# The first x on two hardware queues: a batched matmul on one core

## The chip, the core and the metric

The kernel runs on one core of a Trainium2 chip. The metric is the device time of one execution in microseconds. "Before" is 514.33 us (median of 3 runs, 514.29 to 514.34). A ratio below is the mean time of one kernel's fast runs over the mean of the other's fast runs of the same rounds, so it is not quite the ratio of the medians that stand beside it.

## The reference

```python
batch, m, k, n = 32, 512, 1024, 768
x      = randn(batch, m, k)   # float32
weight = randn(batch, k, n)   # float32
return np.matmul(x, weight).astype(np.float32)
```

There are 32 independent products. x and the weights are 167.8 MB, the output is 50.3 MB.

## The kernel before

Row p of SBUF holds rows 4p to 4p+3 of a batch of x, so a "row tile" is one of four groups of 128 rows. x has to be transposed on PE before it can be multiplied. A transfer "lands" with the last increment of its semaphore, and a "ring" is one queue as a DMA engine sees it. Batch 0 is loaded in float32 from SyncE's hardware queue. All other x and all weights come from GpSimd's software queue, which casts them to bf16 on the way.

```python
x_pool = ctx.enter_context(tc.tile_pool(name="x", bufs=3))
w_pool = ctx.enter_context(tc.tile_pool(name="w", bufs=4))
# ... cut: other pools, views, load_pair, load_w (all on nc.gpsimd) ...

x_first = x_pool.tile([P, MT - 1, K], F32, name="x_sb")     # row tiles 0 to 2
x_fourth = one_pool.tile([P, 1, K], F32, name="one_sb")     # row tile 3
nc.sync.dma_start(x_first, x_view[0, :, :MT - 1])
few = [slice(at, first + 20, 4) for first in (0, 20, 40) for at in range(first, first + 4)]
for rows in (slice(64, 96), slice(96, 112), slice(112, P), slice(60, 62), slice(62, 64), *few):
    nc.sync.dma_start(x_fourth[rows, 0], x_view[0, rows, MT - 1])
load_w(0)
# ... cut: identity matrix ...
load_pair(1); load_w(1); load_w(2); load_pair(3)

for b in range(B):
    # ... cut: loads of x and stores of finished pairs, all on nc.gpsimd ...
    if b + AHEAD < B:                      # AHEAD = 3: waits until weight b-1 is used up
        load_w(b + AHEAD)
    if b == 0:
        xT = {mt: transpose_first(mt) for mt in range(MT - 1)}
    # ... cut: transposes of later batches ...
    for pair in range(2):
        pm = banks()
        for half in range(2):
            mt = 2 * pair + half
            if mt not in xT:               # the fourth tile of batch 0
                xT[mt] = transpose_first(mt)
            matmuls(pm, half, xT[mt], b, range(KT), False)
        evacuate(b, pair, pm)
```

The fourth tile is cut into 17 pieces. Its pieces of 5 rows (12 of them) and of 2 rows go to few DMA engines, which will matter below.

## Time and profile before

| what | before |
|---|---|
| median | 514.33 us |
| span in the profile | 512.6 us |
| PE busy | 84% of the span |
| DMA engines' packets, both queues | 100.6% of 16 engines' span |
| PE starts on x / first product / fourth tile | 10.22 / 15.87 / 42.90 us |
| weight 0 lands | 15.83 us |
| PE's waits for weights after 150 us | 28.7 us in 9 waits |
| last store: issued / last semaphore increment | 503.43 / 511.64 us |

The lines themselves are in the prediction.

### The profile page before, as it was taken

The numbers are of one execution on the slowest core, as the hardware profiler recorded it, in microseconds if no ns is written. First come the engines' busy times: TensorE is split into PE (matmuls) and PEld (weight loads), VectorE is DVE, ScalarE is ACT, GpSimd is POOL, SyncE is SP. The second block draws the span as 40 slices with busy tenths as digits, with TensorE's granted clock in tenths as the row PEclk, the third lists the DMA queues.
The fourth block names the chain that finished last, engine by engine and source line by source line (L and its number), as shares of the span: only waits on it lengthen the run. The fifth ranks groups of instructions, "written<-read, shape, count | busy, mean of one in ns | idle before, by whom it ended". The sixth has DMA issues, their size and how long they took to land.

```text
span 512.6 us, 5733 instructions
## 1 busy us (share of the span) xinstructions
PE 431.9 (84%) x2528; PEld 278.5 (54%) x2576; DVE 130.0 (25%) x196; ACT 76.2 (15%) x129; POOL 37.0 (7%) x69
## 2 busy tenths in 40 slices
PE   2806999999999996997979989897897979999992
PEld 1504666666666563664636546464464645666561
DVE  1203223241415140231413204151050410514130
ACT  1100121212121201111111101111111111111210
POOL 3000010101010101001010000101001000010000
PEclk9956999999999998998989979999798997999998
DMA  8999999999999999999999999999999999999998
GB/s 241 223 221 213 218 218 218 333 220 308 245 219 333 217 323 234 226 326 221 328 225 234 318 224 332 217 246 307 221 333 216 258 295 219 331 219 216 322 427 339
DMA packets 12136, 135.63 MB, mean 265 GB/s; under 512 B 1232, under 2 KB 1232, under 8 KB 2128
## 3 DMA queue, kind: packets, MB, share of 16 engines
q0 software_dynamic: 10864, 126.88, 96.5%
q1 hardware_dynamic: 1248, 8.39, 4.1%
q8 instruction: 20, 0.33, 0.2%
q14 instruction: 4, 0.03, 0.0%
HBM read 167.77 MB, written 50.33 MB: 426 GB/s over the span
## 4 chain that ended last, share of the span: by engine, by line
PE 46%; DMA 37%; issue 8%; DVE 5%; another core or an unknown queue 2%; POOL 1%; ACT 0%; SPq 0%; POOLq 0%
PE pm L123 40%; DMA w_sb<-in_weight_dram 29%; DMA one_sb<-in_x_dram 8%; PE pt L78 5%; DVE xT L85 4%; DVE out_sb L144 1%; PE pt L105 0%; POOL out_dram L164 0%; POOL x_sb L60 0%; POOL w_sb L70 0%; DVE one_sb L144 0%; DVE xT L93 0%; ACT out_sb L145 0%; SPq L151 0%
## 5 line engine op out<-in xcount | busy, mean ns | idle before, releaser
L123 PE MATMUL pm<-w_sb,xT 128*128 128x256 bf16 (+1 forms) x2000 | 349.7, 334 | 31.2 <-DMA w_sb<-in_weight_dram 28.7
L123 PEld LDWEIGHTS <-xT 128*128 128x128 bf16 x2048 | 204.6, 100 | 171.8 <-DMA w_sb<-in_weight_dram 32.2
L144 DVE COPY out_sb<-pm 128x512 f32<-128x512 f32 x62 | 42.9, 692 | 318.3 <-PE pm L123 318.3
L78 PE MATMUL pt<-ident,x_sb 128*128 128x128 f32 x496 | 79.8, 303 | 10.4 <-DVE xT L85 10.1
L78 PEld LDWEIGHTS pt<-ident,x_sb 128*128 128x128 f32 x496 | 69.3, 209 | 21.5 <-DVE xT L85 18.7
L85 DVE COPY xT<-pt 128x1024 bf16<-128x1024 bf16 x120 | 77.4, 687 | 11.0 <-PE pt L78 11.0
L143 ACT COPY out_sb<-pm 128x512 f32<-128x512 f32 x62 | 36.3, 585 | 267.4 <-PE pm L123 267.4
L145 ACT COPY out_sb<-pm 128x512 f32<-128x512 f32 x62 | 36.3, 585 | 151.1 <-PE pm L123 151.1
L70 POOL DMA_DIRECT2D w_sb<-in_weight_dram x33 | 18.0, 546 | 406.4 <-PE pm L123 405.6
L105 PE MATMUL pt<-ident,one_sb 128*128 128x128 f32 x8 | 1.9, 422 | 19.0 <-DMA one_sb<-in_x_dram 19.0
L106 DVE CAST xT<-pt 128x512 bf16<-128x512 f32 x8 | 5.9, 732 | 34.8 <-PE pt L105 34.3
L105 PE MATMUL pt<-ident,x_sb 128*128 128x128 f32 x24 | 5.8, 426 | 10.2 <-DMA x_sb<-in_x_dram 10.2
L105 PEld LDWEIGHTS pt<-ident,one_sb 128*128 128x128 f32 x8 | 1.6, 219 | 19.4 <-issue 19.4
L105 PEld LDWEIGHTS pt<-ident,x_sb 128*128 128x128 f32 x24 | 4.4, 214 | 11.2 <-issue 10.2
L164 POOL DMA_DIRECT2D out_dram<-out_sb x14 | 10.1, 719 | 0.4 <-issue 0.3
L60 POOL DMA_DIRECT2D x_sb<-in_x_dram x15 | 8.1, 539 | 11.2 <-PE pt L105 11.2
L144 DVE COPY one_sb<-pm 128x512 f32<-128x512 f32 x2 | 1.4, 692 | 9.0 <-PE pm L123 9.0
L93 DVE COPY xT<-pt 128x1024 bf16<-128x1024 bf16 x4 | 2.6, 686 | 0.2 <-PE pt L78 0.2
L145 ACT COPY one_sb<-pm 128x512 f32<-128x512 f32 x2 | 1.2, 586 | 4.2 <-PE pm L123 4.2
L143 ACT COPY one_sb<-pm 128x512 f32<-128x512 f32 x2 | 1.2, 585 | 3.8 <-PE pm L123 3.8
L143 ACT ACT_TABLE_LOAD x1 | 1.3, 1283 | 0.7 <-PEq L230 0.7
L64 POOL DMA_DIRECT2D x_sb<-in_x_dram x1 | 0.5, 536 | 0.0
(6 smaller groups left out, 0.9 us busy)
## 6 DMA issues: line engine op xcount, KB each, us to landing
w_sb<-in_weight_dram POOLq DMA_DIRECT2D x31, 1536.0 KB, 41.7
out_dram<-out_sb POOLq DMA_DIRECT2D x14, 3072.0 KB, 55.8
x_sb<-in_x_dram POOLq DMA_DIRECT2D x15, 2048.0 KB, 50.2
out_dram<-out_sb SPq DMA_DIRECT2D x2, 1536.0 KB
x_sb<-in_x_dram SPq DMA_DIRECT2D x1, 1536.0 KB
w_sb<-in_weight_dram POOLq DMA_DIRECT2D x2, 768.0 KB, 48.8
out_dram<-one_sb SPq DMA_DIRECT2D x2, 768.0 KB
out_dram<-out_sb SPq DMA_DIRECT2D x2, 768.0 KB
```

What stands on the lines that cost most here:

```text
L60: nc.gpsimd.dma_start(out=xs[b], in_=pair_view[b // 2])
L70: nc.gpsimd.dma_start(out=ws[b][:, at:at + n, :], in_=w_view[b, :, at:at + n, :])
L78: nc.tensor.transpose(pt[:, j, :], pairs[:, mo, j::JT], ident)
L85: nc.vector.tensor_copy(both[:, :, :, :, half, :].rearrange("p b j i r -> p j b i r"), words(b, mt + MT * half).rearrange("p j (b i r) -> ...
L93: nc.vector.tensor_copy(xT.rearrange("p j m r -> p (j m r)"), words(B - 1, mt).rearrange("p j m -> p (j m)"))
L105: nc.tensor.transpose(pt[:, i, :], rows[:, JT * h + i::KT], ident)
L106: nc.vector.tensor_copy(xT[:, 2 * h:2 * h + 2].rearrange("p j m r -> p j r m"), pt.rearrange("p (j r) m -> p j r m", r=2),)
L123: nc.tensor.matmul(pm[bank][:, at:at + size], xT[:, ko // 2, :, ko % 2], ws[b][:, ko, off:off + size], start=(ko == 0 and not (together an ...
L143: nc.scalar.copy(o[:, 0:512], pm[0])
L144: nc.vector.tensor_copy(o[:, 512:1024], pm[1])
L145: nc.scalar.copy(o[:, 1024:N2], pm[2])
L164: nc.gpsimd.dma_start(out=two_view[at], in_=twos[at])
```

## The change

The intent is to begin the first x on two hardware queues at once, so that PE can start on tile 0 sooner. Two pieces of the fourth tile are also merged.

```diff
-        nc.sync.dma_start(x_first, x_view[0, :, :MT - 1])
+        nc.scalar.dma_start(x_first[:, 1:], x_view[0, :, 1:MT - 1])
+        nc.sync.dma_start(x_first[:, 0], x_view[0, :, 0])
         few = [...]
-        for rows in (slice(64, 96), slice(96, 112), slice(112, P), slice(60, 62), slice(62, 64), *few):
+        for rows in (slice(64, 96), slice(96, P), slice(60, 62), slice(62, 64), *few):
             nc.sync.dma_start(x_fourth[rows, 0], x_view[0, rows, MT - 1])
```

## The prediction

> **What bounds the kernel now.** I read the page's summary first, then the busy time by stretches, then PE's waits after 150 us, then the opening of the timeline. The summary names the bound:
>
> ```profile
> PE 431.9 (84%) x2528; PEld 278.5 (54%) x2576; DVE 130.0 (25%) x196; ACT 76.2 (15%) x129; POOL 37.0 (7%) x69
> DMA  8999999999999999999999999999999999999998
> q0 software_dynamic: 10864, 126.88, 96.5%
> q1 hardware_dynamic: 1248, 8.39, 4.1%
> HBM read 167.77 MB, written 50.33 MB: 426 GB/s over the span
> ```
>
> PE is busy for 84%, but the 16 DMA engines are at 90% or more in every slice except the first and the last, and the two queues together took 96.5 + 4.1 = 100.6% of the engines' span (packets overlap slightly). The software queue is issued by GpSimd: all weights and all x from batch 1 on, with a cast to bf16 on the way. The hardware queue is SyncE's: batch 0's x and the last stores.
>
> Next the stretches (columns: stretch, length, busy us of each engine, granted clock, DMA share, GB/s on the SBUF side, where a cast counts as half of what HBM gave):
>
> ```profile
> 2.00:6.00 4.00, 0.00 (x0) 0.00 (x0) 0.00 (x0) 0.02 (x1) 3.09 (x7) 1.00 0.87 307
> 6.00:16.00 10.00, 5.78 (x25) 4.70 (x26) 3.67 (x5) 0.00 (x0) 0.00 (x0) 1.00 1.05 245
> 16.00:43.00 27.00, 7.91 (x49) 4.63 (x49) 1.43 (x2) 1.75 (x3) 0.53 (x1) 0.69 1.03 221
> 100.00:485.00 385.00, 345.53 (x2023) 221.68 (x2060) 102.87 (x156) 60.07 (x103) 27.79 (x48) 0.95 1.02 263
> 485.00:503.00 18.00, 17.33 (x107) 11.12 (x108) 4.45 (x8) 3.31 (x7) 0.00 (x0) 1.00 1.01 427
> ```
>
> From 2 us to 503 us DMA has no hole. In 16 to 43 us PE works 7.91 of 27 us and DMA still runs at 1.03: PE may stand still there without DMA running out of work. Each transfer lies in a long backlog:
>
> ```profile
> w_sb<-in_weight_dram POOLq DMA_DIRECT2D x31, 1536.0 KB, 41.7
> x_sb<-in_x_dram POOLq DMA_DIRECT2D x15, 2048.0 KB, 50.2
> ```
>
> A weight lands 41.7 us after its issue (the least of all is 14.6 us, for the first), although consecutive landings in the trace are only 7.3 us apart (3.15 MB of HBM reads, 431 GB/s). And the waits of PE from 150 us on:
>
> ```profile
> PE pm L123 <- DMA w_sb<-in_weight_dram: 28.7, 9, 5.5
> ```
>
> Nine waits, 28.7 us, the last until 423.7 us, when weight 26 lands. So PE follows DMA until 423.7 us, and after that DMA is still full: the last store is issued at 503.43 us and its last semaphore increment comes at 511.64 us, 8.2 us later, while 768 KB alone take 1.84 us at the pace of the landings there (507.94, 509.80, 511.64). Both ends of the tail hang on the DMA stream. The time is: start of the stream, plus its work, plus little.
>
> The opening, where the change is:
>
> ```profile
> 0.74 0.38 SPq L151 DMA_DIRECT2D x_sb<-in_x_dram  x1
> 1.27 0.68 POOL L70 DMA_DIRECT2D w_sb<-in_weight_dram  x1 [0.82 <-POOLq L230]
> 10.22 5.84 PE L105 MATMUL pt<-ident,x_sb 128*128 128x128 f32 x24 [10.22 <-DMA x_sb<-in_x_dram]
> 15.87 8.00 PE L123 MATMUL pm<-w_sb,xT 128*128 128x512 bf16 x47
> 42.90 1.94 PE L105 MATMUL pt<-ident,one_sb 128*128 128x128 f32 x8 [19.03 <-DMA one_sb<-in_x_dram]
> ```
>
> The transposes wait for all three row tiles until 10.22 us, because they come as one transfer with one semaphore. The first product, at 15.87 us, starts right after weight 0 lands (15.83 us). The fourth tile comes in 17 pieces and holds PE until 42.90 us.
>
> **What the Trainium skill says.** "DMA: Bandwidth & Descriptors", section "Issuing engines are not separate DMA queues": transfers from any issuer run on the same 16 engines and interleave; a second issuer saves only issue time. The trace agrees as far as it can: one full set of engines, and an issue of 0.38 us before 6 us of moving. The same page, "Queues, rings and completion order": each DMA engine takes turns between the queues at packet granularity. The trace agrees: from 8 to 16 us, while a weight packet takes 925 ns, each engine completes about one small hardware packet per weight packet. Same page, "Rules for kernel authors": "Doesn't help" stands against spreading DMAs over issuers for bandwidth. No run yet shows it here. "Perfetto Trace Analysis", section "DMA Optimizations", says that splitting transfers may finish a task sooner if the DMA engines are generally idle. In this trace they are not, so what it promises can hold only in the first 6 us. On the cost of small packets I go by the trace: 460 ns for 12,288 B and 159 to 172 ns for 4,096 B.
>
> **The change part by part.** Bytes do not change: 167.77 MB read, 50.33 MB written. The instruction order differs only in one issue more on ScalarE, before its table load, and one less on SyncE.
>
> *Issue.* SyncE's first issue took 0.38 us and ScalarE is free at the same 0.7 us. The first packet starts at 1.77 us now; one semaphore step of the start gates both engines, so it stays about there. Gain 0.0. The table load moves by some 0.4 us; ScalarE's first copy is at 18.60 us, so that is hidden.
>
> *More, smaller packets.* Batch 0's first three tiles were 128 packets of 12,288 B, 8 per DMA engine. They become 8 of 8,192 B and 8 of 4,096 B. From 234 ns for 6,144 B and 460 for 12,288 B, a packet costs about 8 ns plus 36.8 ns per KB; a packet after a change of queue seems to cost 13 ns more (172 against 159). That is 8 x (8 + 13), about 0.17 us per DMA engine, at most.
>
> *Ramp.* These 128 packets took 577 ns on average, against 460 at best, because until 5.84 us only this one queue runs (weight 0's first packet) and the rate there was 356 GB/s. The excess is 117 ns x 8 = 0.94 us per engine. If a second ring keeps more requests in flight, part of this can be won; all of it is the ceiling. If the excess is congestion of 16 engines starting at once, nothing is won. I take a third: 0.3 us.
>
> *The merged piece* (rows 96 to 128 in one instead of two transfers of 16 rows): one 22 ns semaphore packet less per engine. Nothing.
>
> *Order in the opening.* The two rings take turns, so tile 0 does not come three times sooner: 8 packets of each ring are done together, at about 6 to 7 us instead of 8.8, and with the 1.2 us to the semaphore PE begins at about 8 us, not 10.2. Weight 0 still lands at about 16, so the first product stays at about 15.9. The fourth tile's large pieces stand behind 0.5 MB instead of 1.5 MB, and part goes out before 5.84 us: about three turns of 1 us fewer, so PE resumes at about 40 us instead of 42.9. Both are PE time, in a stretch where PE is not the bound: weight 4 is issued at 48.78 us now behind a backlog that lasts until 68.10 us, so 3 us earlier moves no byte. PE waits that much longer at its DMA waits after 150 us.
>
> Sum: -0.3 (ramp) + 0.1 (packets) = -0.2 us. 514.33 - 0.2 = 514.1 us.
>
> **The rivals.** First, the early start of PE carries through: 2.9 us, or 0.6%, to 511.4 us. For it speaks only the chain of waits, which runs through the fourth tile at the start; against it the full DMA in 16 to 43 us and the nine later waits, which absorb any lead. Second, the second ring lifts the first 4 us to the steady rate: -0.9 us, 513.4. The 427 GB/s of the last stores, on one hardware ring, speak against one ring being the limit, but those write to HBM. Third, the rings hamper each other or delay weight 0: three queues in turn give it a third of the turns for a while. Weight 0 may be 1 us late, but then something else is 1 us early; the stream is as long. With the packet cost and a worse ramp I come to +0.5 us, 514.8.
>
> **Range and chances.** The ceiling of the gain and the worst of the packet cost give 513.4 to 514.8; 0.1 to 0.2 us more on each side for another chip or run: 513.3 to 515.0. Two per cent are 10.3 us, ten times all that the first x can cost; so within 2% is 0.98, and 0.01 for each side.
>
> **What would show it right or wrong.** Right: transposes from about 8 us, first product still near 16, the fourth tile's transposes near 40, DMA share 1.0 from 2 to 503 us, PE's waits for weights after 150 us grown by about the lead (28.7 to some 31), the last wait still ending at 423 to 424 us. Wrong on the ramp: the DMA share and GB/s in 2 to 6 us rise or fall clearly and every later landing shifts by the same. Wrong on the bound: PE's waits do not grow and the end moves by microseconds.

## The result, and the profile after

The changed kernel takes 514.38 us (median of 4 runs, 514.35 to 514.65), against 514.34 us of the kernel before in the same rounds. The ratio is 1.0002, with a 95% interval of 0.9984 to 1.0019: the same.

The summary of the changed kernel (busy us, DMA by slices, queues) has a third queue, q10, which is ScalarE's:

```profile
PE 435.2 (85%) x2576; PEld 278.3 (54%) x2576; DVE 129.8 (25%) x196; ACT 76.2 (15%) x129; POOL 37.0 (7%) x69
DMA  8999999999999999999999999999999999999998
q0 software_dynamic: 10864, 126.88, 96.5%
q1 hardware_dynamic: 1232, 7.34, 3.6%
q10 hardware_dynamic: 144, 1.05, 0.5%
```

The three queues sum to 100.6% again. The 3 us more of PE are not more work: 48 matmul records are missing in the trace of before (2528 against 2576).

The same stretches as in the prediction (100 to 485 us, again at a DMA share of 1.02 and 263 GB/s, is left out):

```profile
2.00:6.00 4.00, 0.00 (x0) 0.00 (x0) 0.00 (x0) 0.45 (x1) 3.10 (x7) 1.00 0.98 333
6.00:16.00 10.00, 5.42 (x26) 4.23 (x27) 4.16 (x6) 0.00 (x0) 0.53 (x1) 0.98 1.02 240
16.00:43.00 27.00, 10.35 (x54) 6.09 (x53) 0.71 (x2) 1.75 (x3) 0.00 (x0) 0.69 1.04 224
485.00:503.00 18.00, 16.43 (x104) 10.47 (x101) 4.65 (x7) 3.51 (x6) 0.00 (x0) 1.00 1.02 431
```

In the first stretch the rate seems to be up, from 307 to 333 GB/s. It is not: the view counts each DMA record in the stretch in which it starts, and ahead of 2.00 us the kernel before had started 12 records of 12,288 B, the changed one 8 of 4,096 B. Counted from 0 us, before and then after, the rates are alike:

```profile
0.00:6.00 6.00, 0.00 (x0) 0.00 (x0) 0.00 (x0) 1.28 (x1) 4.03 (x12) 1.00 0.71 229
0.00:6.00 6.00, 0.00 (x0) 0.00 (x0) 0.00 (x0) 1.28 (x1) 4.03 (x12) 1.00 0.70 227
```

From 6 to 16 us the rate is down from 245 to 240. From there on nothing differs that could move the end.

The opening of the changed kernel in order of time, and PE's waits after 150 us:

```profile
0.74 0.40 ACTq L151 DMA_DIRECT2D x_sb<-in_x_dram  x1
0.74 0.38 SPq L152 DMA_DIRECT2D x_sb<-in_x_dram  x1
8.97 3.65 PE L105 MATMUL pt<-ident,x_sb 128*128 128x128 f32 x16 [8.97 <-DMA x_sb<-in_x_dram]
15.56 9.64 PE L123 MATMUL pm<-w_sb,xT 128*128 128x512 bf16 x48 [1.40 <-DMA w_sb<-in_weight_dram]
41.85 1.94 PE L105 MATMUL pt<-ident,one_sb 128*128 128x128 f32 x8 [16.65 <-DMA one_sb<-in_x_dram]
```

```profile
PE pm L123 <- DMA w_sb<-in_weight_dram: 28.8, 10, 4.9
```

Both issues start at 0.74 us, as the change wants. PE starts on x 1.25 us sooner (8.97 against 10.22), then has a new wait of 1.40 us for weight 0, and the first product comes 0.31 us sooner. The fourth tile comes 1.05 us sooner. Of that, 0.7 us is left when weight 4 is issued (48.10 against 48.78 us), and none of it reaches a landing. The trace has the landing of every load and store of the software queue, and set side by side they show what became of it: weight 0 lands 0.31 us sooner than before, the next x 0.31 us later, from there to 115 us every transfer 0.2 to 0.3 us later, and those from 124 us up to 467 us between 0.04 us sooner and 0.2 us later. (The experiment with PE held back by 5 us, further down, has the opening of the kernel before, and from 124 us on its landings lie 0.4 us before to 0.6 us after those, so that differences of this size say nothing there.) At the last DMA wait of PE that both kernels share, the landing is at 423.70 us (before: 423.65).

The tail shows it once more. PE happened to finish 1.06 us sooner in this profile, so the last store was issued at 502.37 us instead of 503.43. Its last increment still came at 511.92 us, against 511.64.

### The profile page after: what moved, and what is told of

It reads as the page before. It is cut to its first block, busy times and chain, and to the rows that moved or that the text cites. A ratio compares the mean times of both kernels' runs of the same rounds, so it can differ in the third digit from the quotient of the medians.

```text
span 512.8 us, 5782 instructions
## 1 busy us (share of the span) xinstructions
PE 435.2 (85%) x2576; PEld 278.3 (54%) x2576; DVE 129.8 (25%) x196; ACT 76.2 (15%) x129; POOL 37.0 (7%) x69
## 3 DMA queue, kind: packets, MB, share of 16 engines
q10 hardware_dynamic: 144, 1.05, 0.5%
## 4 chain that ended last, share of the span: by engine, by line
PE 49%; DMA 36%; DVE 5%; issue 5%; another core or an unknown queue 2%; POOL 1%; SPq 0%; ACT 0%; POOLq 0%
PE pm L123 43%; DMA w_sb<-in_weight_dram 28%; DMA one_sb<-in_x_dram 6%; PE pt L78 5%; DVE xT L85 4%; DMA x_sb<-in_x_dram 2%; DVE out_sb L144 1%; PE pt L105 0%; POOL out_dram L165 0%; POOL x_sb L60 0%; POOL w_sb L70 0%; DVE one_sb L144 0%; DVE xT L93 0%; SPq L155 0%
## 5 line engine op out<-in xcount | busy, mean ns | idle before, releaser
L123 PE MATMUL pm<-w_sb,xT 128*128 128x256 bf16 (+1 forms) x2048 | 353.7, 336 | 30.2 <-DMA w_sb<-in_weight_dram 30.2
L78 PE MATMUL pt<-ident,x_sb 128*128 128x128 f32 x496 | 79.8, 302 | 10.5 <-DVE xT L85 10.2
```

Of the source, the lines that this page charges most:

```text
L78: nc.tensor.transpose(pt[:, j, :], pairs[:, mo, j::JT], ident)
L123: nc.tensor.matmul(pm[bank][:, at:at + size], xT[:, ko // 2, :, ko % 2], ws[b][:, ko, off:off + size], start=(ko == 0 and not (together an ...
```

## The experiments

There are two theories to tell apart. The first is the prediction's: the DMA stream sets the end, so PE's opening has slack, and who issues the first x does not matter. The rival is that PE's opening is on the path, as the chain of waits suggests, so that a better arrangement of the first x would pay.

### One queue instead of two (e1_one_queue)

```diff
 # against the changed kernel
-        nc.scalar.dma_start(x_first[:, 1:], x_view[0, :, 1:MT - 1])
         nc.sync.dma_start(x_first[:, 0], x_view[0, :, 0])
+        nc.sync.dma_start(x_first[:, 1:], x_view[0, :, 1:MT - 1])
```

> Tile 0 and then tiles 1 and 2 as two transfers, both from SyncE; the rest as in the changed kernel. Theory (the DMA stream sets the end, whoever issues): 514.3 to 514.5 us, as both kernels. On one ring the transfers go in order, so tile 0 lands well before 8.97 us, by an estimate from 0.5 MB at about 330 GB/s behind 1.77 us plus 1.2 us to the semaphore at about 4.6 us; PE starts there and the end does not move. If the second ring lifted the rate in 2 to 6 us (307 before, 333 after), it falls back to about 307 here; if the smaller packets did it, it stays at about 333. Rival (an earlier start of PE carries to the end): about 4 us faster than the changed kernel, near 510.

Measured: 514.53 us (514.41 to 514.70, 5 runs), before in the same rounds 514.52; ratio 1.0002 (0.9988 to 1.0016). The stretch from 0 to 6 us, and PE's opening:

```profile
0.00:6.00 6.00, 0.58 (x3) 0.61 (x4) 0.00 (x0) 1.28 (x1) 4.02 (x12) 1.00 0.71 224
5.42 1.94 PE L105 MATMUL pt<-ident,x_sb 128*128 128x128 f32 x8 [5.42 <-DMA x_sb<-in_x_dram]
11.23 3.90 PE L105 MATMUL pt<-ident,x_sb 128*128 128x128 f32 x16 [3.88 <-DMA x_sb<-in_x_dram]
15.75 9.86 PE L123 MATMUL pm<-w_sb,xT 128*128 128x512 bf16 x47 [0.62 <-DMA w_sb<-in_weight_dram]
```

Two things follow. For its own aim, the second queue is the worse choice: one queue serves its transfers in order, so PE has tile 0 at 5.42 us instead of 8.97; the two rings take turns, and there tile 0 lands (8.83 us) only 1.55 us before the two other tiles (10.38 us). And the test of the rate, 307 or 333 GB/s from 2 to 6 us, was none: this kernel has 328, but it too had started only 8 records of 4,096 B before 2 us, and from 0 to 6 us it moves 224 GB/s, no more than the 229 of the kernel before. PE's start 4.8 us before that of the kernel before moves nothing, because the first product waits for weight 0 (15.75 us).

### The merged piece alone (e3_merge_only)

```diff
-(slice(64, 96), slice(96, 112), slice(112, P), ...)
+(slice(64, 96), slice(96, P), ...)
```

> The kernel before with only the merged piece of the change: rows 96 to 128 in one transfer instead of two of 16. Theory: one semaphore packet of 22 ns less per DMA engine and one place fewer in the order of SyncE's issues: 514.3 to 514.5 us, fourth tile within 1.5 us of 42.9. No rival gives it more than 0.1 us.

Measured: 514.52 us (514.24 to 516.80, 6 runs) against 514.45 us; ratio 1.0007 (0.9993 to 1.0021). The merge is worth nothing that can be measured. The profile fell on an execution of 515.0 us span with a lower granted clock, and is of use for another reason:

```profile
core 0: 515.0 us, clock 0.842
PE 468.8 (91%) x2528; PEld 290.1 (56%) x2576; DVE 130.3 (25%) x196; ACT 76.2 (15%) x129; POOL 36.9 (7%) x69
PE pm L123 <- DMA w_sb<-in_weight_dram: 0.4, 1, 0.4
```

The last line is PE's waits from 100 us on. At a clock of 0.842 instead of 0.938 PE has next to no waits left and the kernel becomes PE-bound, yet it is only 2.4 us longer. PE is thus a close second bound. The same trace shows which of the two sets the end at the usual clock. PE's slower pace puts the issues of weights up to 17.3 us later than before, and up to 467 us no landing moves by more than 0.6 us. At the end the last store but one lands at 509.71 us (before: 509.79), DMA then stands still until the last store is issued at 510.81 us, and that one lands 3.25 us later, at 514.06. In the kernel before it lands 8.2 us after its issue, so PE could have been some 5 us later there (an estimate from these two figures). What the change did is read from the runs at the usual clock.

### PE held back by 5 and by 16 us (e4_pe_late_6us, e5_pe_late_24us)

These two touch no DMA. Idle transposes, whose result nobody reads, are put on PE after those of the fourth tile: 36 in the first kernel, 144 in the second.

```diff
                     if mt not in xT:
                         xT[mt] = transpose_first(mt)
+                        for _ in range(9):        # 36 in the second kernel
+                            idle = tpsum.tile([P, JT, P], F32, name="pt")
+                            for i in range(JT):
+                                nc.tensor.transpose(idle[:, i, :], x_fourth[:, 0, i::KT], ident)
```

> The kernel before with 36 idle transposes on PE after the fourth tile's, about 6.1 us at 0.17 us each (8 took 1.35 us in the trace), no DMA changed. Theory: the smallest slack of PE against the DMA backlog in this stretch is weight 5, issued at 64.86 us behind a landing at 75.39 us, so 10.5 us; 6 us less of it moves no byte: 514.3 to 514.5 us. Rival (PE's time at the start is on the path): 520.4.

> The same with 144 idle transposes, about 24.5 us. Theory: this exceeds the slack of 10.5 us by 14 us, DMA then runs dry, and the time grows by those 14 us plus some 1 to 4 us until the stream is full again: 528 to 533 us, and DMA share falls visibly between 60 and 100 us. Rival one (PE's start on the path from the first us): 538.8. Rival two (PE is never on the path): 514.4.

Measured: 514.49 us (514.37 to 514.78, 5 runs) for the small delay, ratio 1.0001 (0.9988 to 1.0013); 526.97 us (526.58 to 527.57, 4 runs) for the large one, ratio 1.0244 (1.0230 to 1.0258); before 514.52 us. The idle transposes, the issue of weight 5, and the stretch from 43 to 100 us, first of the small and then of the large delay:

```profile
44.87 5.97 PE L215 MATMUL pt<-ident,one_sb 128*128 128x128 f32 x36
69.80 0.53 POOL L70 DMA_DIRECT2D w_sb<-in_weight_dram  x1 [15.53 <-PE pm L123]
43.00:100.00 57.00, 55.35 (x336) 38.82 (x343) 16.62 (x25) 8.19 (x14) 4.61 (x8) 0.95 1.01 242
```

```profile
44.85 16.93 PE L215 MATMUL pt<-ident,one_sb 128*128 128x128 f32 x144
80.74 0.53 POOL L70 DMA_DIRECT2D w_sb<-in_weight_dram  x1 [15.54 <-PE pm L123]
43.00:100.00 57.00, 55.39 (x378) 43.19 (x384) 15.25 (x23) 5.85 (x10) 2.85 (x5) 0.97 0.88 178
```

The small delay moves the issue of weight 5 from 64.86 to 69.80 us and its landing by 0.06 us. The large one was less than planned (144 transposes took 16.9 us, 0.12 each, not 0.17), and still DMA ran dry: its share falls from 1.01 to 0.88, and weight 5 lands 8.63 us later. The time of 526.97 us is below the 528 to 533 I expected, for a delay that was a third smaller than planned.

This gives an estimate of the slack. Issued at 80.74 us into an empty queue, weight 5 landed at 91.28, so 10.54 us after its issue. In the kernel before it lands at 82.65 us, so by the same 10.54 us it could be issued as late as 72.1 us without loss: 7.3 us later than it is. No run has a delay between 5.2 and 13.4 us that would test it closer. I had reckoned 10.5 us, leaving out the time to fill an empty queue. The growth of 12.4 us is made of 8.6 us at weight 5, another 1.8 us at the x behind it, and some 2 us that come in later along the stream; the last part I cannot assign.

So both simple rivals fall. PE's opening is not on the path within a slack of about 7.3 us, and it is beyond.

### The stream started late (e7_stream_late)

```diff
+        nc.vector.memset(x_first, 0.0)
         nc.sync.dma_start(x_first, x_view[0, :, :MT - 1])
```

> The kernel before; VectorE first fills the tile of batch 0's first three row tiles with zeros, so that SyncE's first transfer has to wait for it. Nothing else moves. Theory: the stream's start counts one to one. With a fill of 2 to 4.4 us (estimate: 3072 columns at the pace of the 512-column casts, 0.73 us each, is 4.4 us at most) the first packet comes that much later than 1.77 us, but weight 0 still begins near 5.8 us; the stream loses the bytes of the hole, about 307 of 430 GB/s by time: +1.5 to +3.5 us, 515.8 to 517.9. Rival (the start is hidden by later waits): 514.4.

Measured: 523.71 us (522.33 to 523.77, 4 runs) against 514.45; ratio 1.0172 (1.0159 to 1.0186). My expectation, 515.8 to 517.9, was wrong. The fill, the issue, the first transposes, the first product, the fourth tile, and the stretch from 43 to 100 us:

```profile
1.45 2.62 DVE L151 MEMSET x_sb<- 128x3072 f32 x1 [1.45 <-PEq L231]
4.10 0.38 SPq L152 DMA_DIRECT2D x_sb<-in_x_dram  x1
21.53 5.43 PE L105 MATMUL pt<-ident,x_sb 128*128 128x128 f32 x24 [21.53 <-DMA x_sb<-in_x_dram]
26.80 7.96 PE L123 MATMUL pm<-w_sb,xT 128*128 128x512 bf16 x47
55.92 1.94 PE L105 MATMUL pt<-ident,one_sb 128*128 128x128 f32 x8 [21.16 <-DMA one_sb<-in_x_dram]
43.00:100.00 57.00, 42.52 (x250) 28.57 (x255) 15.92 (x24) 6.45 (x11) 2.86 (x5) 0.85 0.92 197
```

The x was issued only 3.4 us later, but PE started 11.3 us later. The trace says why: with no x in its way, weight 0's first packet starts at 2.65 us instead of 5.84, and lands 1.65 us sooner; the x, now second, starts at 7.74 us and shares the engines packet by packet with weight and x of the software queue until 19.9 us. The stream itself began only 0.88 us later (2.65 against 1.77). But PE's delay was 13.4 us at weight 5, more than the slack of 7.3 us: by the number of the previous experiment it should land 13.4 - 7.3 = 6.1 us later, and it landed 6.10 us later (again it was issued into an empty queue, and landed 10.47 us after its issue). The rest of the 9.3 us comes in as in the experiment before: 1.3 us at the next x and some 2 us along the stream. Holding x back thus cost little by the stream and much by PE. It also corrects one reading of mine: weight 0 is late in the opening because x is before it, not because its own start takes that long.

### The fourth tile in one transfer (e6_fourth_whole)

```diff
-        for rows in (slice(64, 96), slice(96, 112), slice(112, P), slice(60, 62), slice(62, 64), *few):
+        for rows in (slice(0, P),):
```

> The kernel before with the fourth row tile in one transfer of 128 rows instead of 17 pieces. PE then starts on it soon after 16 us instead of 42.9: a lead of some 25 us. Theory (DMA bound): the lead is lost in the later waits for weights, which grow from 28.7 us to about 54. The 60 rows that went to few DMA engines are spread over all 16, so the others carry 4 packets of 172 ns more: +0.7 us, 515.0. Rival (PE's start on the path): 489.

Measured: 515.97 us (515.77 to 516.52, 5 runs) against 514.45; ratio 1.0029 (1.0016 to 1.0042). The fourth tile, the first wait of PE for a weight, and all such waits from 28 us on:

```profile
23.57 1.04 PE L105 MATMUL pt<-ident,one_sb 128*128 128x128 f32 x8
33.65 16.64 PE L123 MATMUL pm<-w_sb,xT 128*128 128x512 bf16 x99 [0.21 <-DMA w_sb<-in_weight_dram]
PE pm L123 <- DMA w_sb<-in_weight_dram: 41.2, 13, 4.4
```

PE has a lead of 19.3 us here (23.57 against 42.90 us) and the kernel is 1.5 us slower. The rival of 489 us cannot live with that. The waits for weights grew by 12.5 us rather than by the 25 I expected; PE was also busy 7.4 us longer (439.3 against 431.9 us, with 2528 records in both traces), which took most of the rest; why, I did not follow.

The loss of 1.5 us is twice what I expected, and the trace shows its form. Every transfer of the software queue ends with 16 increments of its semaphore, one per DMA engine. For weight 27 in the kernel before, three engines are 2.7 to 3.0 us ahead of the last and the other thirteen lie within 1.2 us; it lands at 430.92 us. With the fourth tile whole, eight engines are 4.1 to 5.2 us ahead, and it lands at 433.44 (one weight earlier: 3.1 to 4.1 us ahead, and 1.4 us late). The mean of the 16 increments is nearly the same (429.8 and 430.2 us). So, as I read it, the small pieces put work on engines that would otherwise run ahead, and the end is set by the slowest engine, not by the mean. This rests on the increments alone: the trace does not name the engine of a record.

### An attempt at a better version (e8_85_rows)

```diff
-        for rows in (slice(64, 96), slice(96, 112), slice(112, P), slice(60, 62), slice(62, 64), *few):
+        for rows in (slice(85, 117), slice(117, P), slice(0, 85)):
```

> An attempt at a better version, from the kernel before: the fourth tile as 32 rows, 11 rows and 85 rows. If 85 rows, as 5 times 17, go to 5 DMA engines in one transfer, the other engines carry about 1 packet of 172 ns less each than before and the five about 3 more: 514.1 to 514.3 us, and the fourth tile lands earlier than 42.9 us because one transfer does not pay a semaphore turn per piece. If the end is set by those five engines instead: 514.7 to 515.0.

Measured: 514.99 us (514.98 to 515.29, 5 runs) against 514.45; ratio 1.0011 (0.9999 to 1.0023). The 85 rows did go to five engines (five late increments, 33.9 to 34.1 us), and PE got the tile 8.7 us sooner:

```profile
34.20 1.95 PE L105 MATMUL pt<-ident,one_sb 128*128 128x128 f32 x8 [9.67 <-DMA one_sb<-in_x_dram]
```

But those five engines were then 2.5 to 3.0 us behind the others at weight 1 (1.4 to 1.8 us in the kernel before), and weight 27 lands 1.05 us later. By the medians it is half a microsecond slower, with an interval that still touches no difference. It is no better version.

### Two queues with whole packets (e2_two_queues_whole_rows, e9_halves_one_queue)

To have two queues without smaller packets, the partitions are halved. The second kernel issues both halves from one queue.

```diff
-        nc.sync.dma_start(x_first, x_view[0, :, :MT - 1])
+        nc.scalar.dma_start(x_first[:P // 2], x_view[0, :P // 2, :MT - 1])   # nc.sync in e9
+        nc.sync.dma_start(x_first[P // 2:], x_view[0, P // 2:, :MT - 1])
```

> The kernel before with its packets of 12,288 B left whole, the 128 partitions halved between SyncE and ScalarE. If the second ring lifts the opening rate: 2 to 6 us at 330 GB/s or more, as after. If the smaller packets did it: about 307. Time 514.1 to 514.5 us in both cases. Rival (two queues double the opening rate or more): some 2 us less by the stream, 512.5.

> The two halves of 64 partitions of the second experiment, which cost 2.8 us, but both from SyncE, one behind the other, with the same packets of 12,288 B. If the halving itself slows the packets[...]: the opening stays slow, 2 to 6 us near 243 GB/s, weight 0 lands about 3 us late, 517 us. If it was two queues with halves running side by side: the opening is back at about 307 GB/s and the time at 514.3 to 514.6 us.

Measured: 517.33 us (516.35 to 518.00, 5 runs) from two queues against 514.52, ratio 1.0054 (1.0041 to 1.0066); 516.60 us (516.23 to 518.04, 5 runs) from one queue against 514.59, ratio 1.0049 (1.0035 to 1.0062). The stretch from 0 to 6 us, two queues and then one:

```profile
0.00:6.00 6.00, 0.00 (x0) 0.00 (x0) 0.00 (x0) 1.28 (x1) 4.03 (x12) 1.00 0.70 162
```

```profile
0.00:6.00 6.00, 0.00 (x0) 0.00 (x0) 0.00 (x0) 1.28 (x1) 4.02 (x12) 1.00 0.72 160
```

The expectation of the first one (514.1 to 514.5) was wrong, and the second shows that it is the halving that costs: the DMA engines are as busy as in the kernel before (0.70 and 0.72, against 0.71) and move almost a third less (162 and 160 against 229 GB/s). Averaged over stretches of 2 us from 1 us on, a packet of 12,288 B takes 650 to 870 ns in the halves from one queue and 740 to 1030 ns from two; in the kernel before it takes 845 ns in the first stretch and then 473 to 530. Weight 0 lands 3.05 us late with two queues and 1.30 us with one, so the second queue may add to it; but the difference between the two medians is within their ranges, and the two profiles fell on the slowest execution of the one kernel (518.0 us) and the fastest of the other (516.2). Nor did the two queues work side by side here: SyncE's half starts its records from 2.07 to 5.07 us, and ScalarE's, issued at the same 0.74 us, from 5.25 to 11.43 us. So no run shows two queues with whole packets at once. Why a half is slow, the traces do not tell. These two also show what the theory asks for: work lost by the stream in the opening is not made up. Weight 0's delay of 3.05 us is still 2.96 us at 424 us, and the time grew by 2.8 (by 3.6 in the span of the profiled execution).

## Why the prediction was right

*The bound.* Right, and now shown from both sides: leads of PE of 1, 9 and 19 us at the fourth tile gain nothing (the last two with other shares for the DMA engines), a delay of 5 us loses nothing, one of 16 us loses 12.4 us, and packets made slower in the first 12 us carry to the end. At the tail the argument was less exact than it looked. A store of 768 KB issued into an idle queue took 3.25 us to land, not the 1.84 us that the pace of landings gave, so of the 8.2 us some 5 were queue. And the 427 GB/s from 485 to 503 us were not those of one hardware ring, since the software queue still ran beside it; from 503 to 509 us, where it ran alone, the rate was 412 GB/s.

*The ramp (-0.3 us) and the packets (+0.1 us).* Neither shows in the time. Summed over the records that start in the first 6 us, the time above the undisturbed length of each size (159, 309 and 460 ns) was 0.91 us per DMA engine before (0.86 to 0.94 in four more runs with the same first transfer), 0.71 us after and 0.83 us with one queue. So some 0.2 us of the ramp may have been won, but by 6 us no more had been moved (227 against 229 GB/s): by these sums what was won in the ramp went into the greater number of packets, which had been reckoned at up to 0.17 us. The sign that was named for a wrong ramp, GB/s in 2 to 6 us and all later landings shifted by the same, came only in its first half, and that was the edge of the view. The landings, 0.2 us later from 51 to 115 us and 0.05 us later at 424 us, show no gain either. The predicted sum of -0.2 us is not seen: the medians differ by +0.04 us, and a tenth of a microsecond cannot be resolved by these runs. The range of 513.3 to 515.0 us held the time of the kernel before, so that the measured time supports the bound, not the sum.

*The rivals.* The interval of the measured ratio stands for 513.5 to 515.3 us. The first rival, 511.4 us, is far outside it. The second, 513.4 us, is just outside, and the bytes moved by 6 us speak against it. The third, rings that hamper each other (514.8 us), is not excluded by the time; no such loss is seen in the landings, which are 0.3 us later at most up to 115 us.

*The order in the opening.* That tile 0 does not come three times sooner was right; 8 us was 8.97 us. The two rings are not quite done together: their last packets of the first x end at 7.31 and 8.84 us. The fourth tile was predicted near 40 us and came at 41.85. The step that was too large is "about three turns of 1 us fewer": set landing against landing, the second large piece came at 15.35 us against 16.46 for the last large piece before, which is one turn.

*PE's waits after 150 us* were to grow to some 31 us and did not (28.8). The lead at weight 4 was only 0.7 us, and the waits of single stages differ by 1 to 3 us between the two traces in both directions, so a growth of that size cannot be seen in one profile. Nor was the wait that ends at 423.7 us the last one: the changed kernel has one more, of 1.29 us until 451.68 us.

*The slack.* "A backlog that lasts until 68.10 us" was the right reason for weight 4, but the tightest place is weight 5, and its slack is about 7.3 us.

*Weight 0 in the opening.* It was taken as starting at 5.84 us by itself. The late-start experiment shows 2.65 us without x before it.

## What to carry to other kernels

When the DMA engines have no hole from start to end, a faster beginning of compute is worth nothing as long as each load is issued before the queue would run dry; measure that slack (landing before, minus issue, minus the 10.5 us of an idle queue here) rather than trust the chain of waits. Two queues are not the way to have the first part of a transfer early: one queue in order brought tile 0 in 3.6 us sooner than two. Once DMA is full, look at the spread of the 16 increments at a landing, because here the end moved with the slowest engine and not with the mean. And before a rate over a short stretch is believed, move the edge of the stretch: 307 against 333 GB/s from 2 us on was 229 against 227 from 0 us on.

## What the Trainium skill lacked or had wrong

- "DMA: Bandwidth & Descriptors", section "Specifications", gives about 358 GB/s as the HBM limit of one core, without the condition that the same page has under its measurements, that this is the share when both cores of a pair stream. This kernel moves 426 GB/s of HBM reads and writes over its whole span, with one core at work.
- The same page, "Rules for kernel authors", says of two transfers to disjoint partition halves that they serialize and are not worth it. The two queues did go one after the other here (2.07 to 5.07 and 5.25 to 11.43 us). But the halves are worse than that: they cost 2.0 us from one queue and 2.8 us from two, with packets of 12,288 B at 650 to 870 ns instead of some 473.
- The same page, "Queues, rings and completion order", has the engine drain a packet of several descriptors before it turns to the next ring. The records in the trace take turns one by one in number: from 9 to 14 us the software queue has 80 weight records and SyncE's has 80, of which 48 are data (172 ns against 925 ns) and 32 semaphore records. Whether a record is a packet or a descriptor is not shown. In the opening, a ring that came second waits much longer: weight 0, issued at 1.27 us, starts at 5.84 us behind x and at 2.65 us without it; and x, issued at 4.10 us behind weight 0, starts at 7.74 us. In the changed kernel, though, the two rings of the first x run side by side from 2.22 us on. Which rule gives all this is open.
- No page gives the size of the imbalance between DMA engines in a long stream: taking 60 rows of 4 KB off a few engines and spreading them let eight engines run up to 5.2 us ahead and cost 1.5 us.
